# Second layer's gate and pooling weights: rounded by their transfer, low parts by an adding transfer

## The chip, the cores and the metric

One core of one Trainium2 chip runs the whole kernel. The metric is device microseconds of one execution; three runs of the kernel before gave a median of 670.25 us (670.14 to 670.65).

## What is computed

A trunk of two encoder layers on a sequence of 512 tokens with 1024 channels, in float32, and a last RMSNorm. Cut to what matters here:

```python
def hybrid_layer(x, ...):
    h = rmsnorm(x, norm_w)
    proj = jnp.einsum('bsd,de->bse', h, w_in)          # 1024 -> 4608 columns
    aq, ak, av, ag, bq, bk, bv, bg, cu, cg = jnp.split(proj, splits, axis=-1)
    o_a = diff_attention(aq, ak, av, ...) * silu(ag)   # 4 heads
    o_b = retention(bq, bk, bv, ...) * silu(bg)        # 4 heads
    o_c = multiscale_pool(cu, ...) * silu(cg)          # 4 channel groups
    return x + jnp.concatenate([o_a, o_b, o_c], -1) @ w_out
```

The columns of the gates bg and cg and of the pooling input cu are, of each layer's input weights, those from 3072 to 4608, twelve blocks of 128 columns.

## The kernel before, in words

**Split numbers.** TensorE multiplies in a rounded 32-bit format (fp32r). So that no precision is lost, each operand is kept as two tiles, a rounded high part and a low part, which is the value less its high part. `split` (L451) makes them: ScalarE rounds the source into the high tile, then VectorE subtracts that from the source into the low tile. `mm3` (L496) is then three matmuls, high by high, high by low and low by high.

**Weights.** `weight_granules` (L38) lists all weights in the order in which they are used, in granules of 128 partitions by 1024 floats (512 KB); one granule is 8 blocks of 128 by 128 for a column block of the input projection. `emit_granule` (L427) takes the next one: SyncE loads it into a raw tile (`wraw`, two buffers), and `split` makes `wh` and `wl` (five buffers each, `WBUFS`, L25). `take` (L443) hands granules out and keeps five emitted ahead, so a granule reuses the buffer of one about five before it, once TensorE is done with that. A raw load needs only a raw tile, so it can run before the weight buffer is free; a raw tile is free again when VectorE has subtracted.

**Use.** `proj_T` (L512) takes one granule and runs 24 matmuls (8 blocks by three) into one of three PSUM banks called `pj`. `gate` (L769) makes a gate from such a bank with ScalarE and VectorE. `c_pool` (L899) copies a bank to a tile `u`, whose margins GpSimd fills with zeros, and makes window sums of it on VectorE. `b_qk` and `b_head` are the retention heads; `headnorm` (L535) raises a row of means to the power -1/2 on GpSimd, sends it through DRAM and scales by it.

**Order.** `ORDERS` (L32) gives the units of each layer by hand; of the second it begins "bv bg0 cu0 bqk0 cg0 bqk1 B0 bg1 cg3 Cy0 cg2 cu1 cu2 cu3 cg1 Cy2 Cy1 bg2 B1 bg3 oT0". Instructions are first recorded in that order. Then `schedule` (L220) simulates five engines with the durations of `cost` (L323) and the delays of `LATENCY` (L162): each engine takes, of what can start at its next free moment, the instruction of the best priority, which is its place in the record less a boost (`HIGH`, L59: +300 for bqk, -20 for cu and cg, -300 for bg). Tiles and banks of a tag are given out in the order of the record, so a unit can hold a bank before it runs. The result is one fixed order for each engine, down to single matmuls, and on the chip each engine keeps it and waits by semaphores. Units therefore mix: eight matmuls of cu0 run first in the second layer, then bqk0's 24 break in, and bg0 runs late.

All instructions are issued from one line, L1055, so the views tell them apart by the tiles they write and read (`wl<-wraw,wh` is a weight's subtraction, `wh<-wraw` its rounding, `pj<-hh,wh` a projection's matmul).

Of the kernel before, what the change touches and what calls it, by code (L numbers as in the profile page):

```python
# [9 lines left out]
F32 = mybir.dt.float32  # L10
F32R = mybir.dt.float32r
AF = mybir.ActivationFunctionType
ALU = mybir.AluOpType
# [10 lines left out]
AQ, AK, AV, AG, BQ, BK, BV, BG, CU, CG = 0, 512, 1024, 1536, 2048, 2304, 2560, 3072, 3584, 4096  # L24
WBUFS = 5  # L25
# [12 lines left out]
def weight_granules():  # L38

    out = []  # L40
    for l in range(DEPTH):
        for u in ORDERS[l]:
            if u in ("bv", "av"):
                out += [("w_in", l, (256 * g, BV if u == "bv" else AV), (2, 512)) for g in range(4)]
                continue
            kind, i = u[:-1], int(u[-1])
            if kind in ("bg", "ag", "cu", "cg"):
                out.append(("w_in", l, (0, {"bg": BG, "ag": AG, "cu": CU, "cg": CG}[kind] + i * P), (8, P)))
            elif kind in ("bqk", "qk"):
                out += [("w_in", l, (0, c + i * P), (8, P)) for c in ((BQ, BK) if kind == "bqk" else (AQ, AK))]  # L50
            elif kind[0] == "o":
                out += [("w_out", l, ("PQRSTU".index(c) * 256, 512 * i), (2, 512)) for c in kind[1:]]
    return out
# [5 lines left out]
HIGH = {"A": 3000, "Am": 300, "B": 3000, "t": 150, "av": -20, "qk": 60, "o": 150, "bqk": 300, "Cy": 2000, "cu": -20, "bg": -300, "cg": -20, "ag": -20}  # L59
# [110 lines left out]
class Recorder:  # L170
# [9 lines left out]
    def add(self, name, engine, method, args, kw):  # L180
        op = Op()
        op.engine, op.method, op.args, op.kw = engine, (name, method), args, kw
        op.prio, op.unit = len(self.ops) - self.boost, self.unit
        outs = [args[0]] + ([kw["accum_out"]] if "accum_out" in kw else [])
        ins = [v for v in list(args[1:]) + [x for k, x in kw.items() if k != "accum_out"] if isinstance(v, View)]
        deps, bases = {}, []
        for views, write in ((ins, False), (outs, True)):
            for v in views:
                if not isinstance(v, View):
                    continue  # L190
                b, m = v.base, v.mask()
                if b not in bases:
                    bases.append(b)

                def hits(entries):
                    return [e for e in entries if e[1] < v.p1 and v.p0 < e[2] and e[3] & m]

                for e in hits(b.writes) + (hits(b.reads) if write else []):
                    if e[0] is not op:
                        deps[id(e[0])] = e[0]  # L200
                entry = (op, v.p0, v.p1, m)
                if write:
                    def covered(e):
                        return v.p0 <= e[1] and e[2] <= v.p1 and not e[3] & ~m and e[0] is not op
                    b.writes = [e for e in b.writes if not covered(e)] + [entry]
                    b.reads = [e for e in b.reads if not covered(e)]
                else:
                    b.reads.append(entry)
        if engine == "PE":
            b = outs[0].base  # L210
            if b.chain is not None:
                deps[id(b.chain)] = b.chain
            b.chain = op
        for b in bases:
            b.left += 1
        op.bases, op.deps, op.users = bases, list(deps.values()), []
        op.time, op.hold = cost(engine, method, args, kw)
        self.ops.append(op)

# [103 lines left out]
def cost(engine, method, args, kw):  # L323

    out = args[0]
    n = out.idx.size if isinstance(out, View) else 0
    psum = any(isinstance(a, View) and a.base.space == "psum" for a in args)
    if engine == "PE":
        if method == "transpose":
            return 109, 109  # L330
        f32 = args[1].base.dt == F32 and not any(s[0] == "bitcast" for s in args[1].steps)
        if f32:
            return 2 * 110 + 4 * n * 0.417, 2 * 110 + 4 * n * 0.417
        t = max(107, n * 0.417) + 2.5
        return t, t
    if engine == "SP":
        nbytes = (out.p1 - out.p0) * n * 4 if isinstance(out, View) and out.base.space != "dram" else P * D * 4
        if isinstance(out, View) and out.base.space == "dram":
            nbytes = 16384
        return nbytes / 360.0, 475  # L340
    if engine == "DVE":
        if method == "tensor_tensor":
            t = 1.041 * n + 69
        elif method == "scalar_tensor_tensor":
            t = 1.041 * n + (130 if isinstance(args[2], View) else 69)
        elif method == "tensor_scalar":
            t = (1.17 if psum else 0.64) * n + 69
        elif method == "tensor_copy":
            t = (1.04 if psum else 0.521) * n + 68
        elif method == "reciprocal":  # L350
            t = 6.2 * n + 69
        elif method == "memset":
            t = 9
        else:
            t = 1.041 * max(n, 2) + 75
        return t, t
    if engine == "ACT":
        t = 0.833 * n + (52 if psum else 94)
        for k in ("bias", "scale"):
            t += 93 * isinstance(kw.get(k), View)  # L360
        t += 93 * ("accum_out" in kw)
        return t, t
    if method == "tensor_tensor" and kw["op"] == ALU.pow:
        return 300 + 164 * n, 300 + 164 * n
    if method == "tensor_tensor":
        return 60 + 2.2 * n, 60 + 2.2 * n
    return 60 + 1.3 * n, 60 + 1.3 * n


def record(ins: dict, out: bass.AP):  # L370
    nc = Recorder()
    x_d = ins["x"][0]

    def sb(tag, shape, bufs=1, dt=F32, name=None):
        return nc.tile("sb", tag, shape, bufs, dt)
# [45 lines left out]


    granules = [(i, shape) for i, (_, _, _, shape) in enumerate(weight_granules())]
    wt = []
    wstate = [0]

    def emit_granule(parts=1):  # L427
        at, (nk, nc_) = granules[len(wt)]
        shp = [P, nk, nc_]
        src = ins["wg"][at].rearrange("p (k c) -> p k c", k=nk)  # L430
        raw = sb("wraw", shp, 2)
        hi = sb("wh", shp, WBUFS, F32R)
        lo = sb("wl", shp, WBUFS, F32R)
        n = shp[1] // parts
        for i in range(parts):
            k = slice(i * n, (i + 1) * n)
            was, nc.boost = nc.boost, HIGH.get("w", 0)
            nc.sync.dma_start(raw[:, k, :], src[:, k, :])
            split(hi[:, k, :], lo[:, k, :], raw[:, k, :])
            nc.boost = was  # L440
        wt.append((hi, lo))

    def take(n):  # L443
        i = wstate[0]
        wstate[0] += n
        while len(wt) < min(i + WBUFS, len(granules)):
            emit_granule()
        return wt[i:i + n]


    def split(dh, dl, src):  # L451
        nc.scalar.copy(dh, src)
        nc.vector.tensor_tensor(dl, src, dh.bitcast(F32), op=ALU.subtract)
# [227 lines left out]
    class Layer:  # L681
# [18 lines left out]
        def first_values(self):  # L700
# [10 lines left out]
            for u in START.split():  # L711
                i = int(u[1:] or 0)
                if u[0] == "k":
# [5 lines left out]
                    if i % 2 == 0:  # L719
                        emit_granule(2 if i < FINE else 1)  # L720
# [316 lines left out]
@with_exitstack  # L1037
def trunk(ctx: ExitStack, tc: tile.TileContext, ins: dict, out: bass.AP):
    pools = {
        "sb": ctx.enter_context(tc.tile_pool(name="sb", bufs=1)),  # L1040
        "psum": ctx.enter_context(tc.tile_pool(name="ps", bufs=1, space=bass.MemoryType.PSUM)),
        "dram": ctx.enter_context(tc.tile_pool(name="dr", bufs=1, space=bass.MemoryType.DRAM)),
    }
    with tc.manual_schedule():
        for op in record(ins, out).schedule():
            for b in op.bases:
                if b.real is None:
                    name = f"{b.tag}_{b.slot}"
                    b.real = pools[b.space].tile(b.shape, b.dt, tag=name, bufs=1, name=name)

            def real(v):
                return v.resolve() if isinstance(v, View) else v

            name, method = op.method
            op.inst = getattr(getattr(tc.nc, name), method)(*[real(a) for a in op.args], **{k: real(v) for k, v in op.kw.items()})  # L1055
# [67 lines left out]
```

## Time and profile before

| | us |
|---|---|
| median of three runs | 670.25 |
| the profiled execution | 670.98 |
| its span, from first to last instruction | 669.2 |
| TensorE busy in the span | 657.1 |
| VectorE busy | 478.3 |
| ScalarE busy | 385.2 |
| GpSimd busy | 30.2 |

Times in the views count from the span's start. PE is TensorE's matmuls, DVE is VectorE, ACT ScalarE, POOL GpSimd, SPq the queue that SyncE issues transfers from. Matmuls are pipelined: one begins 0.23 us after the other though each lasts 0.39, so a stall is read from the distance of two starts. The granted clock of TensorE is 0.999 of its 2.4 GHz over the whole span.

### The profile page before, as it was taken

The numbers are of one execution on the slowest core, as the hardware profiler recorded it, in microseconds if no ns is written. First come the engines' busy times: TensorE is split into PE (matmuls) and PEld (weight loads), VectorE is DVE, ScalarE is ACT, GpSimd is POOL, SyncE is SP. The second block draws the span as 40 slices with busy tenths as digits, with TensorE's granted clock in tenths as the row PEclk, the third lists the DMA queues.
The fourth block names the chain that finished last, engine by engine and source line by source line (L and its number), as shares of the span: only waits on it lengthen the run. The fifth ranks groups of instructions, "written<-read, shape, count | busy, mean of one in ns | idle before, by whom it ended". The sixth has DMA issues, their size and how long they took to land. (4 is left out here: it accounts for less than half of the span.)

```text
span 669.2 us, 8859 instructions
## 1 busy us (share of the span) xinstructions
PE 657.1 (98%) x3173; PEld 538.0 (80%) x3173; DVE 478.3 (71%) x865; ACT 385.2 (58%) x735; POOL 30.2 (5%) x51
## 2 busy tenths in 40 slices
PE   8999999999999999999999999999999999999996
PEld 6887878887788888887888788778888878888885
DVE  5798886776788879875754878587558846887733
ACT  6646885534776776552524877244567756874321
POOL 0100000000000000001010000000100000000011
PEclk9999999999999999999999999999999999999999
DMA  8545454223234322244113414433331243212302
GB/s 309 202 153 165 116 153 111 95 97 103 66 102 122 116 80 63 91 114 123 64 64 111 141 64 96 121 121 84 80 111 59 69 134 109 92 63 81 110 31 95
DMA packets 29300, 71.59 MB, mean 107 GB/s; under 512 B 5460, under 2 KB 9716, under 8 KB 29256
## 3 DMA queue, kind: packets, MB, share of 16 engines
q1 hardware_dynamic: 29256, 71.02, 34.4%
q8 instruction: 25, 0.41, 0.3%
q14 instruction: 19, 0.16, 0.1%
HBM read 68.83 MB, written 2.18 MB: 106 GB/s over the span
## 5 line engine op out<-in xcount | busy, mean ns | idle before, releaser
L1055 PE MATMUL pj<-hh,wh 128*128 128x512 f32 x448 | 176.9, 398 | 2.1 <-DVE gate L1055 1.3
L1055 PE MATMUL pj<-hl,wh 128*128 128x512 f32 x448 | 176.4, 395 | 0.0
L1055 PE MATMUL pj<-hh,wl 128*128 128x512 f32 x448 | 176.0, 396 | 0.0
L1055 ACT CAST wh<-wraw 128x1024 fp32r<-128x1024 f32 (+1 forms) x97 | 100.8, 1039 | 84.3 <-PE pj L1055 65.5
L1055 DVE TENSOR_TENSOR wl<-wraw,wh 128x1024 fp32r<-128x1024 f32 (+1 forms) x97 | 117.3, 1209 | 35.0 <-ACT wh L1055 34.5
L1055 PEld LDWEIGHTS pj<-hh,wh 128*128 128x128 f32 x448 | 84.1, 188 | 21.8 <-DVE gate L1055 1.9
L1055 PEld LDWEIGHTS pj<-hh,wl 128*128 128x128 f32 x448 | 84.0, 188 | 18.3
L1055 PEld LDWEIGHTS pj<-hl,wh 128*128 128x128 f32 x448 | 84.2, 188 | 17.8
L1055 PE MATMUL pj<-wh,mAC 128*128 128x512 f32 (+1 forms) x264 | 86.8, 390 | 0.0
L1055 ACT ACTIVATE soft<-soft,sm 128x512 f32<-128x512 f32 x96 | 68.6, 721 | 21.8 <-DVE sm L1055 20.8
L1055 DVE TENSOR_TENSOR x<-x,pj 128x512 f32<-128x512 f32 (+1 forms) x65 | 43.8, 676 | 19.7 <-PE pj L1055 19.2
L1055 PEld LDWEIGHTS pj<-wh,mAC 128*128 128x128 f32 x264 | 48.8, 188 | 10.3 <-DVE mAC L1055 0.2
L1055 PE MATMUL pj<-wl,mAC 128*128 128x512 f32 (+1 forms) x132 | 51.5, 390 | 0.0
L1055 PE MATMUL lg<-qk 128*128 128x512 f32 (+1 forms) x192 | 50.3, 360 | 0.7 <-DVE soft L1055 0.4
L1055 DVE CUSTOM_DVE_ANT_0 soft<-lg,wide 128x512 f32<-128x512 f32 x64 | 43.1, 686 | 9.7 <-PE lg L1055 7.0
L1055 POOL TENSOR_TENSOR st<-st,neghalf 128x4 f32<-128x4 f32 (+1 forms) x28 | 25.0, 892 | 476.2 <-DVE st L1055 447.5
L1055 PE MATMUL pj<-wh,mB 128*128 128x512 f32 (+1 forms) x136 | 44.3, 382 | 0.0
L1055 PE MATMUL pj<-wh,hh 128*128 128x512 f32 x104 | 41.3, 397 | 0.4 <-DVE vl L1055 0.4
L1055 PE MATMUL pj<-wl,hh 128*128 128x512 f32 x104 | 41.4, 398 | 0.0
L1055 PE MATMUL pj<-wh,hl 128*128 128x512 f32 x104 | 41.1, 396 | 0.0
L1055 PEld LDWEIGHTS lg<-qk 128*128 128x128 f32 x192 | 32.5, 188 | 8.0 <-issue 1.5
L1055 PE MATMUL ov<-T,vh 128*128 128x256 f32 x192 | 38.8, 283 | 0.0
(156 smaller groups left out, 951.6 us busy)
## 6 DMA issues: line engine op xcount, KB each, us to landing
wraw<-in_wg SPq DMA_DIRECT2D x95, 512.0 KB, 3.3
hn<-row SPq DMA_DIRECT2D x16, 256.0 KB, 3.4
wide<-gd SPq DMA_DIRECT2D x8, 448.0 KB, 3.1
T<-in_xT_w SPq DMA_DIRECT2D x8, 258.0 KB, 4.9
x<-in_x SPq DMA_DIRECT2D x8, 256.0 KB, 5.2
wide<-dd SPq DMA_DIRECT2D x8, 256.0 KB, 5.1
out<-T SPq DMA_DIRECT2D x8, 256.0 KB, 2.1
qd<-dd SPq DMA_DIRECT2D x8, 128.0 KB, 4.5
```

Source lines behind the costliest of these rows:

```text
L1055: op.inst = getattr(getattr(tc.nc, name), method)(*[real(a) for a in op.args], **{k: real(v) for k, v in op.kw.items()})
```

## The change

For the twelve granules of the second layer with the gate columns bg and cg and the pooling columns cu, the raw tile falls away. GpSimd issues a transfer from DRAM straight into the high tile, which rounds. ScalarE copies the high tile, times -1, into the low tile. GpSimd then issues a second transfer of the same weights into the low tile, which adds to what lies there. VectorE's subtraction falls away. All other weights go as before, the attention gates ag among them.

The recorder learns that a transfer with `accum_op` also reads its target. The cost table gets an entry for GpSimd's transfers: 5300 ns until done and 600 ns of GpSimd, 7200 and 900 where it adds. The whole order is planned again with that.

```diff
+        kw_ins = [args[0]] if "accum_op" in kw else []
...
+    if engine == "POOL" and method == "dma_start":
+        return (7200, 900) if "accum_op" in kw else (5300, 600)
...
+    BYTRANSFER = [i for i, (name, l, (r, c), _) in enumerate(weight_granules()) if l == 1 and name == "w_in" and BG <= c < CG + 512]
...
+        if at in BYTRANSFER:
+
+            hi = sb("wh", shp, WBUFS, F32R)
+            lo = sb("wl", shp, WBUFS, F32R)
+            was, nc.boost = nc.boost, HIGH.get("w", 0)
+            nc.gpsimd.dma_start(hi, src)
+            nc.scalar.activation(lo, hi.bitcast(F32), AF.Copy, scale=-1.0)
+            nc.gpsimd.dma_start(lo, src, accum_op=ALU.add)
+            nc.boost = was
+            wt.append((hi, lo))
+            return
```

## Rows read from the trace of the kernel before

**Rows 1.** The page, part 1: busy us, share of the span and instructions of each engine.

```profile
PE 657.1 (98%) x3173; PEld 538.0 (80%) x3173; DVE 478.3 (71%) x865; ACT 385.2 (58%) x735; POOL 30.2 (5%) x51
```

**Rows 2.** Busy time by stretch: length, busy time of each engine (instructions), clock, DMA.

```profile
350.00:480.00 130.00, 127.37 (x612) 103.72 (x611) 87.19 (x127) 71.30 (x124) 3.47 (x9) 1.00 0.35 101
480.00:657.50 177.50, 176.63 (x854) 145.46 (x853) 121.83 (x235) 102.74 (x213) 8.77 (x9) 1.00 0.28 87
```

**Rows 3.** TensorE's order of time: start, us, operation, tiles, [idle before <- releaser].

```profile
368.20 0.40 PE L1055 MATMUL pj<-hl,wh 128*128 128x512 f32 x1
369.14 0.50 PE L1055 MATMUL pj<-hh,wh 128*128 128x512 f32 x1 [0.55 <-ACT soft L1055]
...
410.40 0.59 PE L1055 MATMUL lg<-qk 128*128 128x256 f32 x3 [0.40 <-DVE soft L1055]
...
426.59 0.39 PE L1055 MATMUL pj<-hh,wl 128*128 128x512 f32 x1
426.82 0.40 PE L1055 MATMUL pj<-hh,wh 128*128 128x512 f32 x1
428.54 0.50 PE L1055 MATMUL pj<-hh,wh 128*128 128x512 f32 x1 [1.32 <-DVE gate L1055]
...
435.11 0.40 PE L1055 MATMUL pj<-hh,wl 128*128 128x512 f32 x1
435.74 0.50 PE L1055 MATMUL pj<-hh,wh 128*128 128x512 f32 x1 [0.23 <-ACT u L1055]
```

**Rows 4.** Tile wl on VectorE, 350 to 480: ns least/median/most, first and last start.

```profile
L1055 DVE TENSOR_TENSOR wl<-wraw,wh x21: 1215/1225/1227, 354.7 to 479.2; 128x1024 fp32r<-128x1024 f32 x21
```

**Rows 5.** VectorE's order of time ahead of the gate that TensorE waits for.

```profile
426.06 1.22 DVE L1055 TENSOR_TENSOR wl<-wraw,wh 128x1024 fp32r<-128x1024 f32 x1
427.20 0.69 DVE L1055 TENSOR_TENSOR T<-soft,T 128x512 fp32r<-128x512 f32 x1
427.80 0.68 DVE L1055 SCALAR_TENSOR_TENSOR gate<-gate,pj 128x512 f32<-128x512 f32 x1
```

**Rows 6.** ScalarE's order of time.

```profile
353.62 1.05 ACT L1055 CAST wh<-wraw 128x1024 fp32r<-128x1024 f32 x1 [0.85 <-PE pj L1055]
...
366.10 0.62 ACT L1055 CAST pwh<-wraw 128x512 fp32r<-128x512 f32 x1 [3.19 <-DMA wraw<-in_pool_w]
...
434.15 1.05 ACT L1055 CAST wh<-wraw 128x1024 fp32r<-128x1024 f32 x1 [7.95 <-PE pj L1055]
435.11 0.58 ACT L1055 COPY u<-pj 128x512 f32<-128x512 f32 x1
```

**Rows 7.** Waits of SyncE's queue, 350 to 480: us in total, times, longest us.

```profile
SPq L1055 <- DVE wl L1055: 86.4, 19, 17.0
```

**Rows 8.** GpSimd's order of time, two of its powers.

```profile
412.80 1.02 POOL L1055 TENSOR_TENSOR st<-st,neghalf 128x4 f32<-128x4 f32 x1 [28.67 <-issue]
...
460.44 1.01 POOL L1055 TENSOR_TENSOR st<-st,neghalf 128x4 f32<-128x4 f32 x1 [13.26 <-DVE st L1055]
```

**Rows 9.** Transfers of the whole kernel: KB each, median us from issue to landing.

```profile
wraw<-in_wg SPq DMA_DIRECT2D x95, 512.0 KB, 3.3
...
sin<-in_c_sin SPq DMA_DIRECT2D x2, 256.0 KB, 6.6
```

**Rows 10.** SyncE's queue in order of time, one issue.

```profile
411.46 0.33 SPq L1055 DMA_DIRECT2D wraw<-in_wg  x1
```

**Rows 11.** TensorE's order of time at the granules cu0, bg0 and cg3.

```profile
353.14 0.40 PE L1055 MATMUL pj<-wh,hl 128*128 128x512 f32 x1
...
357.55 0.39 PE L1055 MATMUL pj<-hh,wh 128*128 128x512 f32 x1
...
375.04 0.39 PE L1055 MATMUL pj<-hh,wh 128*128 128x512 f32 x1
...
384.26 0.39 PE L1055 MATMUL pj<-hh,wl 128*128 128x512 f32 x1
...
400.13 0.65 PE L1055 MATMUL pj<-hh,wh 128*128 128x512 f32 x2
```

More of the change, by code (lines that the diff above doesn't have):

```diff
@@ L184, in add @@
         outs = [args[0]] + ([kw["accum_out"]] if "accum_out" in kw else [])
-        ins = [v for v in list(args[1:]) + [x for k, x in kw.items() if k != "accum_out"] if isinstance(v, View)]
+        kw_ins = [args[0]] if "accum_op" in kw else []
+        ins = [v for v in list(args[1:]) + [x for k, x in kw.items() if k != "accum_out"] + kw_ins if isinstance(v, View)]
         deps, bases = {}, []
```

## The prediction

> **What bounds the kernel now.** I read first the page's busy times: TensorE is busy for 98% of the span, VectorE for 71%, ScalarE for 58%, GpSimd for 5% [rows 1]. A busy TensorE need not be a full one, so the second view is the busy time by stretch. The weights that the change touches are used between 357 and some 475 us. Of the 130 us from 350 to 480, TensorE is busy 127.37; after that, to 657.5, it is busy 176.63 of 177.50 [rows 2]. There is almost nothing to win outside the first stretch. VectorE, which the change relieves, is busy 87.19 of the 130 us; it has 43 us to spare and bounds only where TensorE waits for it.
>
> The third view is TensorE's order of time, searched for late starts. Matmuls of 512 columns start every 0.23 us (426.59 to 426.82). Three starts of the stretch come later than that [rows 3]:
> - at 369.14, 0.94 after the one before, so 0.71 lost (released by ScalarE);
> - at 428.54, 1.72 after the one before, so 1.49 lost (released by VectorE);
> - at 435.74, 0.63 after the one before, so 0.40 lost (released by ScalarE).
>
> Together 2.60 us. A fourth, at 410.40, idles 0.40 for a VectorE operation of a retention head that no weight stands ahead of. So about 3.0 us can be had at most, under half a per cent of the kernel.
>
> **The change, part by part.** *VectorE loses* twelve subtractions of 1.225 us [rows 4], 14.7 us of busy time. They count only where TensorE ends up waiting behind one. For the 1.49 us, VectorE's order of time shows it: the subtraction at 426.06 is that of cg1, and a split and then the gate operation that TensorE waits for start behind it at 427.20 and 427.80 [rows 5]. Without it both start 1.14 earlier, and the wait shrinks by 1.14. Bounds: 0 to 1.49.
>
> *ScalarE keeps* twelve passes: instead of rounding 1024 columns into the high part it copies them, negated, into the low part; I cost both at the 1.05 us of the rows [rows 6]. What moves is their place: the pass now waits for the first transfer into the weight tile, which itself waits until the buffer is free. At 434.15 ScalarE rounds bg2 the moment its buffer comes free, and the copy of cu1's result that TensorE's bank waits for stands behind it at 435.11. That pass moves at least 3 us later, and the 0.40 goes (bounds 0 to 0.40). At 366.10 ScalarE has just waited 3.19 us for the raw load of the pooling matrices; the copies that TensorE waits for at 369.14 stand behind that. The load waits for one of two raw tiles: SyncE's queue waits 86.4 us in this stretch for VectorE to be done with them [rows 7]. The twelve granules no longer use raw tiles, so this load comes early, and the 0.71 goes (bounds 0 to 0.71).
>
> *SyncE loses* twelve loads; its queue only gets shorter. *GpSimd gains* 24 transfers on an instruction queue that is served in order: behind an adding transfer that waits for ScalarE stand the margin fills of the next pooling input and the powers of the head norms, which VectorE waits for. It has little else to do here; a power takes 1.01 or 1.02 us [rows 8]. A fill that is held up by some 2 us delays a pooling chain, not TensorE: there are three banks, and the one that the pooling input came from is wanted again two granules, 11 us, later. I cost it at 0; with that cover gone it costs the delay itself.
>
> *The new chain.* Before, a raw load ran ahead of the buffer's release, and one pass on ScalarE and one on VectorE (2.3 us) came after it. Now all of it comes after: issue, transfer, ScalarE, issue, adding transfer. No row shows a GpSimd transfer. For an issue, the nearest rows are 0.33 us (a load on SyncE's queue [rows 10]) and 1.01 (GpSimd's power); I take 1.0, as that is GpSimd's own. For the first transfer, 3.3 (the 512 KB weight loads) to 6.6 (the slowest kind of load) [rows 9]; I take 3.3, the same bytes into the same kind of tile. For the adding one, which also reads 512 KB back from the tile, 3.3 to 9.9 (6.6 + 3.3); I take twice 3.3. Sum: 1.0 + 3.3 + 1.05 + 1.0 + 6.6 = 12.95, and four handovers of 0.1 (TensorE's matmul of 353.14 ends at 353.54, ScalarE begins at 353.62 [rows 6, 11]): 13.4 us. Ends: 0.33 + 3.3 + 1.05 + 0.33 + 3.3 = 8.3, and 1.0 + 6.6 + 1.05 + 1.0 + 9.9 = 19.6.
>
> The Trainium skill ("DMA: Bandwidth & Descriptors", section "Anatomy of one DMA — SWDGE (gpsimd) path") fits a transfer issued by GpSimd as 2.0 us plus its bytes over 436 GB/s, which makes an estimate of 3.2 us for 512 KB, without a price for adding. By it the first term would be 3.2 in place of 3.3, and the sum the same; no run so far shows such a transfer.
>
> *Its cover.* Counting 24 matmuls to a granule along TensorE's order, the twelve granules have 19 us or more from the release of their buffer to their first use, but for two. For cg3 it is 15.7 (its buffer's last matmul, at 384.26, ends at 384.65; its own first is the second of the two from 400.13, at about 400.35). For cu0 it is 4.0: its buffer is free at 353.54, its first matmul at 357.55 [rows 11]. A chain of 13.4 is far too late for that. But the planner counts transfers as long and takes up what is ready: bg0, whose buffer was free well before 350 and which holds a bank, though it runs only from 375.04 now; and bqk0, which now breaks into cu0 after eight matmuls. That is 48 matmuls, 11.0 us, so cu0's low part is not missed before 368.6: a cover of 15.1 us. The 13.4 fit under 15.1 and 15.7.
>
> *Sum.* Gains 0.71 + 1.14 + 0.40 = 2.25. ScalarE gets twelve new waits for first transfers, where the plan puts their landing: the one wait of 3.19 seen here cost 0.71, and I take a third of that once, 0.25 (0 to 0.71). Net 2.0 us. The profiled execution took 670.98 with a span of 669.2, so 1.78 lie outside it: 669.2 - 2.0 + 1.78 = 668.98. The median of the runs is 0.73 under the profiled execution: 668.25, so **668.3 us**.
>
> **The rivals.** About 0.2%, 1.34 us, is what a measurement of this kernel can tell from no change, so faster means under 668.9 and slower over 671.6.
>
> 1. *The stalls move.* The whole order is planned anew, and TensorE's small stalls depend on which operation stands ahead of which; new neighbours take back what the old ones gave. For it: VectorE has 43 us idle, and TensorE waits all the same. Against: all three stalls have a cause by name that the change takes away. Time: 2.25 gone, about as much come back, 670.2, within 669.0 and 671.5.
> 2. *The chain outgrows its cover*, at cu0 and cg3. The stalls are (chain - 15.1) + (chain - 15.7). They use up the 2.25 at a chain of 16.5 us, and from 17.2 the kernel is slower by over 0.2%. At 18.4, the middle between that and the upper end: 3.3 + 2.7 - 2.25 = 3.75, so 674.0; at the upper end 4.5 + 3.9 - 2.25, so 676.4. For it: no row has an adding transfer, which could be slower than two loads. Against: 13.4 from the nearest rows.
> 3. *GpSimd's issues wait for VectorE.* If the VectorE operation in progress held up each issue, two waits of up to 1.23 make the chain 15.9: cu0 is 0.8 late and cg3 0.2, so -2.0 + 1.0, 669.2. Against: the power takes the same 1.01 and 1.02 us wherever it lies [rows 8]. The Trainium skill ("SBUF — State Buffer", section "SBUF: two separate sides") warns that GpSimd cannot write descriptors while VectorE runs in a mode that takes both of its ports; for operations with two inputs in SBUF, as nearly all are here, it names only GpSimd's reads as held up.
>
> **How the numbers follow.** Forecast 47%, rival 1 29%, rival 2 20%, rival 3 4%. The forecast's own range is 667.2 (all 3.0 gone) to 668.9. The range starts at 666.9, as another 0.3 may come from the 0.87 us after 480; about 5% lie below. It ends at 673.0, which takes in rivals 1 and 3 and the lower part of rival 2; some 14% lie above. Faster 0.47; same 0.33 (rivals 1 and 3); slower 0.20 (rival 2).
>
> **What would show it.** VectorE has 85 weight subtractions instead of 97 and 14.7 us less. TensorE runs bg0 ahead of cu0 at 357.6, and no start near 369, 428 and 436 is over 0.3 late. From a buffer's release to the end of the adding transfer it is under 15 us, and TensorE waits for no weight tile. I am wrong if TensorE waits for a GpSimd transfer at cu0 or cg3, if ScalarE waits long for first transfers with banks held behind it, or if new late starts of the same size stand elsewhere.

## The result, and the profile after

The changed kernel is slower: 676.34 us (median of 6 executions, 674.04 to 677.78) against 670.58 (6 executions on the same chip, 670.14 to 672.85), a ratio of 1.0076 with a 95% interval of 1.0052 to 1.0099. Its profiled execution took 676.97 us with a span of 675.2, 6.0 more than before.

The page of the changed kernel, parts 1, 3 and 6 (columns as in [rows 1] and [rows 9]; of part 3: packets, MB, share of 16 engines' span). All its instructions are issued from L1071.

```profile
PE 658.7 (98%) x3173; PEld 539.1 (80%) x3173; DVE 465.5 (69%) x853; ACT 384.6 (57%) x735; POOL 46.8 (7%) x75
...
q0 software_dynamic: 3456, 12.58, 8.2%
...
wh<-in_wg POOLq DMA_DIRECT2D x12, 512.0 KB, 4.6
wl<-in_wg POOLq DMA_DIRECT2D x12, 512.0 KB, 6.1
...
wide<-dd SPq DMA_DIRECT2D x8, 256.0 KB, 4.6
```

VectorE has twelve instructions less (865 to 853), and the page's group of weight subtractions falls from 117.3 to 102.6 us. So the relief came in full, and it bought nothing. The windows of the changed kernel say where to look, in the form of [rows 2]:

```profile
350.00:480.00 130.00, 123.50 (x587) 100.19 (x586) 74.01 (x114) 68.65 (x120) 19.34 (x31) 0.99 0.58 140
480.00:657.50 177.50, 176.53 (x852) 145.16 (x851) 121.20 (x233) 104.55 (x214) 8.20 (x8) 1.00 0.27 88
```

TensorE loses 3.87 us of busy time in the first stretch and 0.10 in the second; the DMA engines' busy share there goes from 0.35 to 0.58, though the bytes per second only go from 101 to 140. TensorE's order of time in the changed kernel, its late starts and one ordinary matmul ahead of the first (columns as in [rows 3]):

```profile
367.39 0.40 PE L1071 MATMUL pj<-hh,wl 128*128 128x512 f32 x1
368.61 0.50 PE L1071 MATMUL pj<-hh,wl 128*128 128x512 f32 x1 [0.81 <-DMA wl<-in_wg]
...
400.45 0.50 PE L1071 MATMUL pj<-hh,wh 128*128 128x512 f32 x1 [0.71 <-DVE gate L1071]
...
414.67 0.59 PE L1071 MATMUL lg<-qk 128*128 128x256 f32 x3 [1.38 <-DVE soft L1071]
...
423.62 0.74 PE L1071 MATMUL lg<-qk 128*128 128x256 f32 x4 [2.19 <-DVE soft L1071]
...
451.66 0.50 PE L1071 MATMUL pj<-hh,wh 128*128 128x512 f32 x1 [1.41 <-ACT u L1071]
```

Reckoned as in the prediction, by the distance of two starts less the usual one, these lose 0.98, 0.88, 1.54, 2.35 and 1.57 us, together 7.3. In the kernel before the stretch lost 3.5: the 2.6 of the forecast's three stalls, 0.65 at 410.40 and 0.29 at a start at 418.61. In this execution none of the three old ones is left at its place. Five others came:

- 0.98 at 368.61: cu0's low part. This is rival 2, in small. In a second profiled execution (a_full, the last experiment) it doesn't show, and 0.49 is lost at 369.52 instead.
- 0.88 and 1.57 at 400.45 and 451.66: an operation of the new order that stands too far ahead of its supplier. The planner's own simulation has both holes, with 1.02 and 1.80 us. This is rival 1.
- 1.54 and 2.35 at 414.67 and 423.62: two logits (`lg`) of the retention heads. Nothing in the prediction led there.

The last matmul starts 5.20 us later than before (668.16 against 662.96): 3.8 from the late starts of this stretch, 0.3 less elsewhere, and 1.7 because TensorE ran at the lower of its two clocks, 1.2 GHz, for one piece of 3.42 us:

```profile
424.97:428.39 3.42, 3.42 (x10) 2.65 (x10) 2.61 (x4) 1.48 (x2) 0.87 (x1) 0.50 0.90 122
```

The other 0.8 us lie behind the last matmul, in the end of the kernel (7.05 us there in place of 6.24, and the same 7.05 or 7.06 in every kernel that keeps the new order). The clock piece turned out to be no cost of the change (below, at the last experiment).

**What the heads wait for.** Each retention head masks its logits with a table of decays (`wide<-dd`, 256 KB) that SyncE loads for it. There is one buffer, so the next load is issued when VectorE has used the last one, and a load that lands late makes the next head late. In the kernel before, SyncE's issues and VectorE's first operation behind each load, in order of time:

```profile
405.23 0.38 SPq L1055 DMA_DIRECT2D wide<-dd  x1
409.56 0.69 DVE L1055 SCALAR_TENSOR_TENSOR soft<-lg,wide 128x512 f32<-128x512 f32 x1 [1.07 <-DMA wide<-dd]
...
413.29 0.38 SPq L1055 DMA_DIRECT2D wide<-dd  x1
417.77 1.29 DVE L1055 SCALAR_TENSOR_TENSOR soft<-lg,wide 128x512 f32<-128x512 f32 x2 [0.60 <-DMA wide<-dd]
```

From issue to use 4.3 and 4.5 us. In the changed kernel, the chain that ended last (start, us, what) and then the order of time:

```profile
358.75 9.81 DMA wl<-in_wg
...
407.88 5.93 DMA wide<-dd
...
416.59 6.19 DMA wide<-dd
```

```profile
409.02 0.89 POOL L1071 DMA_DIRECT2D wl<-in_wg  x1 [8.30 <-ACT wl L1071]
412.20 1.84 POOL L1071 DMA_DIRECT2D wl<-in_wg  x2 [2.30 <-ACT wl L1071]
...
413.83 0.69 DVE L1071 SCALAR_TENSOR_TENSOR soft<-lg,wide 128x512 f32<-128x512 f32 x1 [1.68 <-DMA wide<-dd]
...
422.87 1.29 DVE L1071 SCALAR_TENSOR_TENSOR soft<-lg,wide 128x512 f32<-128x512 f32 x2 [2.52 <-DMA wide<-dd]
...
429.74 1.29 DVE L1071 SCALAR_TENSOR_TENSOR soft<-lg,wide 128x512 f32<-128x512 f32 x2 [2.11 <-DMA wide<-dd]
```

The same loads take 5.9 and 6.2 us, and a third, issued at 424.19, 5.5 (5.1 before, where nothing waited for it). Three adding transfers go out beside the first two loads. While the second load is out, from 416.59 to 422.87, GpSimd's queue alone takes most of the 16 engines (part 3 of the page for that window: packets, MB, share):

```profile
q0 software_dynamic: 336, 1.21, 84.4%
q1 hardware_dynamic: 416, 0.26, 19.0%
```

The packet records of the trace show what that does: the load's first packet starts 3.5 us after its issue, while that of the load of 405.23 in the kernel before starts 1.0 us after. In part 4 of the page, the chain that ended last, the loads `wide<-dd` hold 2% of the span by themselves.

### The profile page after: what moved, and what is told of

Same layout as the page of the kernel before. It is cut to its first block, busy times and chain, and to the rows that moved or that the text cites. A ratio compares the mean times of both kernels' runs of the same rounds, so it can differ in the third digit from the quotient of the medians.

```text
span 675.2 us, 8863 instructions
## 1 busy us (share of the span) xinstructions
PE 658.7 (98%) x3173; PEld 539.1 (80%) x3173; DVE 465.5 (69%) x853; ACT 384.6 (57%) x735; POOL 46.8 (7%) x75
## 4 chain that ended last, share of the span: by engine, by line
PE 71%; issue 16%; DMA 5%; DVE 3%; ACT 3%; POOL 1%; POOLq 0%; ACTq 0%; DVEq 0%; SPq 0%
PE pj L1071 58%; PE lg L1071 6%; PE ov L1071 4%; PE tp L1071 4%; DMA wide<-dd 2%; DMA wl<-in_wg 1%; DVE soft L1071 1%; ACT soft L1071 1%; ACT qk L1071 1%; POOL st L1071 1%; DMA hn<-row 1%; ACT T L1071 1%; DMA wide<-gd 0%; DVE T L1071 0%; DVE qk L1071 0%
## 5 line engine op out<-in xcount | busy, mean ns | idle before, releaser
L1071 PE MATMUL pj<-hh,wh 128*128 128x512 f32 x448 | 177.4, 398 | 2.1 <-ACT u L1071 1.4
L1071 PE MATMUL pj<-hh,wl 128*128 128x512 f32 x448 | 176.9, 398 | 0.8 <-DMA wl<-in_wg 0.8
L1071 PE MATMUL pj<-hl,wh 128*128 128x512 f32 x448 | 177.0, 397 | 0.0
L1071 ACT CAST wh<-wraw 128x1024 fp32r<-128x1024 f32 (+1 forms) x85 | 88.1, 1037 | 70.5 <-PE pj L1071 53.4
L1071 DVE TENSOR_TENSOR wl<-wraw,wh 128x1024 fp32r<-128x1024 f32 (+1 forms) x85 | 102.6, 1208 | 28.1 <-ACT wh L1071 27.5
L1071 PEld LDWEIGHTS pj<-hh,wh 128*128 128x128 f32 x448 | 84.5, 189 | 21.7 <-ACT u L1071 2.3
L1071 PEld LDWEIGHTS pj<-hh,wl 128*128 128x128 f32 x448 | 84.4, 189 | 19.4 <-DMA wl<-in_wg 1.3
L1071 PEld LDWEIGHTS pj<-hl,wh 128*128 128x128 f32 x448 | 84.6, 189 | 17.7
L1071 PE MATMUL pj<-wh,mAC 128*128 128x512 f32 (+1 forms) x264 | 86.9, 391 | 0.0
L1071 ACT ACTIVATE soft<-soft,sm 128x512 f32<-128x512 f32 x96 | 68.6, 721 | 21.6 <-DVE sm L1071 20.6
L1071 DVE TENSOR_TENSOR x<-x,pj 128x512 f32<-128x512 f32 (+1 forms) x65 | 43.8, 676 | 20.8 <-PE pj L1071 20.3
L1071 PEld LDWEIGHTS pj<-wh,mAC 128*128 128x128 f32 x264 | 48.8, 188 | 10.6 <-DVE mAC L1071 0.3
L1071 POOL TENSOR_TENSOR st<-st,neghalf 128x4 f32<-128x4 f32 (+1 forms) x28 | 24.1, 861 | 449.5 <-DVE st L1071 446.1
L1071 PE MATMUL lg<-qk 128*128 128x512 f32 (+1 forms) x192 | 50.6, 360 | 3.7 <-DVE soft L1071 3.6
L1071 PE MATMUL pj<-wl,mAC 128*128 128x512 f32 (+1 forms) x132 | 51.7, 392 | 0.0
L1071 DVE CUSTOM_DVE_ANT_0 soft<-lg,wide 128x512 f32<-128x512 f32 x64 | 43.1, 686 | 9.7 <-PE lg L1071 7.0
L1071 PE MATMUL pj<-wh,mB 128*128 128x512 f32 (+1 forms) x136 | 44.3, 382 | 0.0
L1071 PE MATMUL pj<-wh,hh 128*128 128x512 f32 x104 | 41.4, 398 | 0.4 <-DVE vl L1071 0.4
L1071 PEld LDWEIGHTS lg<-qk 128*128 128x128 f32 x192 | 32.5, 188 | 11.4 <-issue 2.9
L1071 PE MATMUL pj<-wl,hh 128*128 128x512 f32 x104 | 41.3, 397 | 0.0
L1071 PE MATMUL pj<-wh,hl 128*128 128x512 f32 x104 | 41.1, 396 | 0.0
L1071 PE MATMUL ov<-T,vh 128*128 128x256 f32 x192 | 38.8, 283 | 0.0
```

## Experiments

Two theories stood against each other. The order theory (A): the new plan places TensorE's work badly, and the transfers themselves are harmless. The transfer theory (B): the new transfers take the 16 DMA engines from loads that TensorE waits for; in its sharper form (B1) it is the adding ones, because adding is dear. The kernels ran in three groups, each on one chip, beside executions of the kernel before on the same chip (medians of those: 672.65, 673.33 and 673.24 us). Ratios are against these, with 95% intervals.

**The order of before, with the new transfers (order_b).** The instructions of the kernel before keep its order on every engine; eleven granules (cu0 is left as it was) get the three new instructions in place of their load, rounding and subtraction.

```diff
-    order = record(ins, out).schedule()
+    order = merged(ins, out)   # order of before; a granule's transfers go in where its buffer comes free
```

> Eleven of the twelve granules (all but cu0) go by GpSimd's two transfers, but every engine keeps the order of the kernel before: TensorE's, VectorE's less eleven subtractions, ScalarE's with the copy put 5.6 us of planned time after the buffer's release. Theory A (the new order is what costs): no new holes, two of the old late starts go, 668 to 670.5 us beside 670.5 of before. Theory B (the transfers are what cost, since they slow the decay-table loads that the retention heads wait for, from 4.3 and 4.5 us to 5.9 and 6.2): the heads' two waits of 1.54 and 2.35 stay although the order is the old one, 673 to 676. Theory C (the chain outgrows its cover): cu0 left out, so 0.98 less than the changed kernel, 675.

Measured: 678.94 us, 1.0098 (1.0075 to 1.0120), above what any of the theories expected. The order of before doesn't bring the time back: a loss of this size needs no new order, and a decay load is late here too. Its order of time on VectorE, TensorE and ScalarE:

```profile
412.16 0.69 DVE L1108 SCALAR_TENSOR_TENSOR soft<-lg,wide 128x512 f32<-128x512 f32 x1 [2.33 <-DMA wide<-dd]
...
412.99 0.71 PE L1108 MATMUL lg<-qk 128*128 128x256 f32 x4 [2.24 <-DVE soft L1108]
...
441.62 1.06 ACT L1108 ACTIVATE wl<-wh 128x1024 fp32r<-128x1024 f32 x1 [3.49 <-DMA wh<-in_wg]
...
446.38 1.06 ACT L1108 ACTIVATE wl<-wh 128x1024 fp32r<-128x1024 f32 x1 [3.22 <-DMA wh<-in_wg]
...
453.95 0.50 PE L1108 MATMUL pj<-mAC,pwh 128*128 128x512 f32 x1 [3.44 <-ACT mAC L1108]
```

The decay load that ends at 412.16 was issued at 404.45 and took 7.7 us, with adding transfers issued at 403.00, 405.66 and 408.36. The second loss is another: ScalarE keeps its order and stands twice for over 3 us before a first transfer; a pooling chain starts late behind that, and TensorE waits 3.44 for its last copy. Two pieces of 3.41 us at the lower clock, from 414.10 and 455.05, are in the time as well. So the total is no measure of the decay loads alone.

**The adding transfer cut to an eighth (a_add8).** The order of the changed kernel is kept exactly; the transfer adds only the first of the 8 blocks, so seven eighths of these low parts are left as the negated high part.

```diff
+            if "accum_op" in op.kw:
+                op.args = [v[:, 0:1, :] for v in op.args]
```

> The changed kernel in its own order, but each adding transfer moves and adds the first of eight blocks alone (seven eighths of the low parts keep the negated high part, so this computes something else). Theory A (order): only cu0's wait of 0.98 goes, 674.5 to 676. Theory B (traffic of the adding transfers slows the decay-table loads): these land in under 5 us again, the heads' waits shrink from 3.9 to about 1 and the stretch at half clock goes, 671 to 672.5. Theory C (the adding transfer is too long): cu0's wait goes, 675 to 675.5.

Measured: 673.87 us, 1.0016 (1.0001 to 1.0031). The order, the first transfers and the number of instructions are the same. cu0's wait is gone, the heads' waits are 0.29 and 0.89 (1.54 and 2.35 in the change), and the decay loads take 4.7, 4.8 and 4.6 us. The two holes of the plan stay, 0.88 and 1.57. It changes nothing but the bytes that are added. The ratio makes the gain look larger than it is: ten of the 25 executions of the kernel before on this chip have a mean granted clock of 0.996 or less, and none of these ten. Among executions at 0.997 or more (those of the kernel before take 672.32 at 0.997 and 672.06 at 0.998, but 674.57 at 0.996) it takes 673.87 against 672.06, 1.8 us longer; the change, on the third chip, takes 3.7 longer (675.96 against 672.29). So about half of the loss is gone.

**The adding transfer without adding (a_addplain).** Order and bytes of the changed kernel; the second transfer overwrites instead of adding, so the low parts hold the rounded weights themselves.

```diff
+            op.kw.pop("accum_op", None)
```

> The changed kernel in its own order, with the second transfer of each granule a plain one of the same bytes: nothing is added, so the low tile ends up as the weights themselves (this computes something else). Theory B1 (adding is what is dear: its 4 KB packets took 328 ns on their DMA engine, a plain transfer's some 160 to 174): between the cut-down kernel and the full change, 0.2 to 0.45% over before, decay loads after 5 us or less. Theory B2 (twelve more transfers of 512 KB are dear, adding or not): as the full change, 0.65 to 0.9%. Theory A (the new order's two holes): 0.65% or more, as the order is the same.

Measured: 674.49 us, 1.0029 (1.0008 to 1.0050). Its page, parts 3 and 6:

```profile
q0 software_dynamic: 3456, 12.58, 6.1%
...
wl<-in_wg POOLq DMA_DIRECT2D x12, 512.0 KB, 3.9
```

The same packets and bytes as in the change take 6.1% of 16 engines' span instead of 8.2%. Over the two spans that is 656 and 886 us of engine time, 230 us more for the 1536 packets that add (twelve transfers of 128 packets of 4 KB): 0.15 us each. The packets' own records agree: a median of 0.33 us for one that adds and 0.17 for one that doesn't; 0.16 for a packet of SyncE's weight loads in the kernel before. The windows from 404 to 432 us show it as occupation, of the kernel before, the change, this kernel and a_add8 in turn (the last two columns are the DMA share and GB/s):

```profile
404.00:432.00 28.00, 26.15 (x145) 21.74 (x145) 20.09 (x31) 14.56 (x29) 1.02 (x1) 1.00 0.47 119
```

```profile
404.00:432.00 28.00, 24.43 (x136) 20.69 (x136) 18.30 (x30) 18.48 (x34) 5.73 (x7) 0.94 0.79 157
```

```profile
404.00:432.00 28.00, 26.10 (x151) 22.23 (x150) 18.21 (x30) 18.26 (x34) 4.28 (x7) 1.00 0.67 175
```

```profile
404.00:432.00 28.00, 27.14 (x156) 22.86 (x155) 19.50 (x32) 18.60 (x34) 5.74 (x7) 1.00 0.54 116
```

The change moves fewer bytes per second than this kernel and keeps the engines busier. The heads' waits follow the kind of transfer: 3.9 us with adding (1.54 + 2.35), 2.2 without (0.69 + 1.53), 1.2 with an eighth (0.29 + 0.89), at one and the same order. They are the load's time and nothing else: in the change, a_full, this kernel and a_add8 the first wait is the time from issue to use of its load (5.9, 6.0, 5.1 and 4.7 us) less 4.4, the second (6.3, 6.4, 5.5 and 4.8) less 3.9.

The same chip ran the change once more (a_full, below): 677.13, 2.6 us above this kernel, and 1.7 above it among executions with a mean clock of 0.997 or more (675.96 against 674.22). So B1, that adding is what is dear, holds for about half of the loss. The rest is not divided by an experiment: at 0.997 or more this kernel is 1.9 us above the kernel before and a_add8 1.8, so the seven eighths of plain bytes between them make no difference that can be told, and both keep the plan's holes and its longer end. Single traces give an account of it: the late starts of the stretch come to 7.0 us in a_full, 4.7 here and 3.6 in a_add8, against 3.5 before, and the end is 0.8 longer in all three. That makes 4.3, 2.0 and 0.9 us beside the measured 3.7, 1.9 and 1.8.

**Part of the granules (a_first3, a_late9).** Only bg0, cu0 and cg0 by transfer, and only the other nine. Both are planned anew.

```diff
-... if l == 1 and name == "w_in" and BG <= c < CG + 512]
+... if l == 1 and name == "w_in" and BG <= c < CG + 512 and c in (BG, CU, CG)]      # a_first3
+... if l == 1 and name == "w_in" and BG <= c < CG + 512 and c not in (BG, CU, CG)]  # a_late9
```

> The changed kernel with only bg0, cu0 and cg0 by transfer; their adding transfers are over by some 375 us, before the heads' decay loads after 400. Theory B: no late decay load, so the time of the kernel before, within 0.2% (the plan has one hole of 0.7 us, cu0 may wait 1 us as in the changed kernel, and 1 or 2 us of the old waits may go): 0.998 to 1.002. Theory C (chain at cu0): cu0's wait of about 1 us is all that is lost. Theory A: holes from bg0 being used up early, up to 0.4% slower.

> The changed kernel without these three: the nine later granules by transfer. Theory B: the adding transfers of cg3, cg2, cu1, cu2 and cu3 still meet the heads, 0.5 to 1.0% slower than before. Theory A with bg0 and cu0 as the cause: as fast as before, within 0.2% (but this plan has two holes of 1.5 us, so up to 0.45% slower). Theory C: no wait at cu0, 0.1% less than the changed kernel.

Measured: 673.18 us, 0.9999 (0.9981 to 1.0017), and 677.61 us, 1.0070 (1.0044 to 1.0095). The three whose transfers end before the heads cost nothing that can be told, the nine around the heads about as much as all twelve. TensorE and VectorE in order of time in a_late9:

```profile
419.43 1.29 DVE L1071 SCALAR_TENSOR_TENSOR soft<-lg,wide 128x512 f32<-128x512 f32 x2 [5.15 <-DMA wide<-dd]
...
420.17 0.73 PE L1071 MATMUL lg<-qk 128*128 128x256 f32 x4 [3.35 <-DVE soft L1071]
```

That load was issued at 412.53 and took 6.9 us. The pair is less clean than it looks, on both sides. In a_late9 the heads' two waits are 0.93 and 3.51, but the plan of this kernel has two holes of its own (1.45 and 1.58 in the planner's simulation), and TensorE loses about 1.3 at each of them, at 455.79 and 457.46. So the heads are only about half of its 8.7 us of late starts.

And the one profiled execution of a_first3 (674.76 us, the longest of its ten) has heads' waits of 1.69 and 2.25 too, with decay loads of 5.1 and 5.7 us and no transfer of GpSimd's in flight. Beside the first of them one of SyncE's own weight loads is on the engines; in the last microsecond before the second is used, hardly a packet moves, and that stays unexplained. So waits of that size come without GpSimd's transfers as well. They cost little here because this plan closes the old stalls at 428 and 436: its late starts are 4.8 us (these two and 0.89 at 395.22) against 3.5 before, and this execution also has a piece of 3.41 us at the lower clock.

**A second buffer for the decay table (a_decay2, and b_decay2 as its control).** Every other head of the second layer loads its table into a tile of its own, in the changed kernel and in the kernel before.

```diff
+        if row >= 4 and row % 2:
+            t = sb("rb", [P, S]).rearrange("p (j c) -> p j c", j=2)
+        else:
             t = sb("wide", [P, 896], 1)[:, 0:512].rearrange("p (j c) -> p j c", j=2)
```

> The changed kernel, in which the second layer's odd retention heads load their decay table into a second buffer, so a load no longer waits for the head before. Both theory A and B put 1.54 + 2.35 of TensorE's waits and the 3.4 us at half clock (1.7) on these loads: if they are the cause, 5 us go and 670.5 to 671.5 is left, with the hole of 0.88 still there; the plan closes the other (1.57) by itself here, which would make it 669 to 670. Theory C (chain of the weights): 675 to 676.

> The kernel before with the same second buffer, as the control: its late starts at the heads are 0.62 and 0.29 (410.4 and 418.6), so at most 0.9 us go, and the plan moves others a little: 669.3 to 670.6. If it gains as much as the changed kernel does, the second buffer is not about the change.

Measured: 676.36 us, 1.0051 (1.0028 to 1.0073), and 672.80 us, 0.9997 (0.9978 to 1.0017). The control costs and gains nothing. In the changed kernel I had expected nearly all of the loss back; the interval overlaps that of the change. What is gone in the trace is the hole of 1.57, which this plan closes by itself. The heads' waits of 3.9 are gone too, but one of 4.1 at 430.25 came in their place, for a gate that stands on VectorE behind a head's masking. Its order of time and its list of issues between 350 and 480 say why:

```profile
413.82 0.87 POOL L1074 DMA_DIRECT2D wl<-in_wg  x1 [2.29 <-ACT wl L1074]
415.31 0.88 POOL L1074 DMA_DIRECT2D wl<-in_wg  x1 [0.61 <-DVE T L1074]
...
425.46 0.69 DVE L1074 SCALAR_TENSOR_TENSOR soft<-lg,rb 128x512 f32<-128x512 f32 x1 [5.73 <-DMA rb<-dd]
```

```profile
rb<-dd SPq DMA_DIRECT2D x1, 256.0 KB, 10.9
```

The load could go out earlier, at 414.40, and for that it went out right between two adding transfers and took 10.9 us. So the single buffer is not the cause of the late load. One of the ten executions, the only one with a mean clock above 0.996, took 672.40; no profile of it shows whether its load was late.

**Transfers added to the kernel before (b_junkadd, b_junkcopy).** For the same twelve granules GpSimd also loads their weights in two halves into a tile that nobody reads, adding or plain.

```diff
+                nc.gpsimd.tensor_copy(junk[:, 0:1], hi[:, 0, 0:1].bitcast(F32))
+                for h in range(2):
+                    nc.gpsimd.dma_start(junk.rearrange("p (k c) -> p k c", k=4), src[:, 4 * h:4 * h + 4, :], accum_op=ALU.add)
```

> The kernel before in its own order, with its own weight chain, and besides, for each of the twelve granules, two adding GpSimd transfers of half a granule into a tile that nobody reads, issued when ScalarE has rounded the granule. Theory B (adding transfers hold the DMA engines, and the retention heads' decay tables arrive late): the decay loads after 400 us take 5.5 us or more in place of 4.3 and 4.5, TensorE's waits at the heads grow by 1.5 to 4 us, 0.3 to 1.0% slower than before. Theory A (order) and C (chain): no change within 0.2%.

> The same kernel with plain GpSimd transfers of the same bytes in place of the adding ones. If it is the adding (packets of 4 KB took 328 ns each in the changed kernel against some 160 to 174 for plain ones), about half or less of the loss is left, up to 0.3%. If any GpSimd traffic does it, as slow as with adding. Theory A and C: no change.

Measured: 696.08 us, 1.0342 (1.0308 to 1.0377), and 678.08 us, 1.0088 (1.0063 to 1.0114), both far above what was expected. Adding is much worse than plain, but this pair is not clean. The waits of b_junkadd (us in total, times, longest):

```profile
POOL rb L1065 <- DMA rb<-in_wg: 81.7, 19, 7.1
...
DVE hn L1065 <- POOL u L1065: 12.9, 2, 7.8
```

GpSimd waits for its own transfers, because all go into one tile, and the margin fills and powers of the pooling units stand queued behind. Plain, the first wait is 59.6 us and the second 3.6. In the profile of b_junkadd TensorE also runs 17.1 us at its lower clock, which is up to 8.5 us lost. How the 23 us divide between a queue held up, that clock and full DMA engines isn't shown, and the pair is left out of the argument.

**Only cg1 and bg2 by transfer (a_cg1bg2).** These are the two granules whose subtraction and rounding the prediction found ahead of the late starts at 428.54 and 435.74.

```diff
+... if l == 1 and name == "w_in" and c in (CG + P, BG + 2 * P)]
```

> Only cg1 and bg2 go by transfer, the two granules whose passes stood ahead of the gate and the copy that TensorE waited for at 428.5 and 435.7 (1.48 and 0.39 us); their transfers start after the heads' last decay load, and the plan has no hole. Theory B: those waits go and nothing new comes, 1.2 to 2 us less than before, 0.997 to 0.9985. Theory A (any new plan moves the stalls): within 0.2% of before on either side.

Measured: 673.09 us, 1.0007 (0.9987 to 1.0028): no gain, against an expected one. The 0.40 at 435.74 is gone. Of the 1.49, this is left, in order of time on VectorE and TensorE:

```profile
424.49 1.29 DVE L1071 SCALAR_TENSOR_TENSOR soft<-lg,wide 128x512 f32<-128x512 f32 x2 [0.65 <-DMA wide<-dd]
425.69 0.68 DVE L1071 SCALAR_TENSOR_TENSOR gate<-gate,pj 128x512 f32<-128x512 f32 x1
...
426.43 0.50 PE L1071 MATMUL pj<-hh,wh 128*128 128x512 f32 x1 [1.87 <-DVE gate L1071]
```

The subtraction of [rows 5] is out of the way, the gate operation starts 2.1 earlier than before (425.69 against 427.80), and TensorE waits 1.87 for it instead of 1.32. It also came to that place earlier, since its matmul before starts at 424.16 instead of 426.82. The gate now stands right behind a head's masking of 1.29 us, which itself idles 0.65 for a decay load. So with the subtraction gone, the next work of the heads in VectorE's order sets the wait.

**The change once more (a_full).** The unchanged changed kernel, as an anchor on the third chip.

> The changed kernel once more, as the anchor on the same chip as the other two: 0.5 to 1.0% over before by all theories; TensorE's two waits at the heads 3 us or more together, with decay loads of 5.5 us and more.

Measured: 677.13 us, 1.0064 (1.0043 to 1.0086). Heads' waits of 1.61 and 2.45, decay loads of 6.0, 6.4 and 5.1 us, and in its windows no piece at the lower clock:

```profile
350.00:480.00 130.00, 123.81 (x595) 100.47 (x594) 74.09 (x114) 68.80 (x120) 19.35 (x31) 1.00 0.58 142
```

cu0's wait is not there, but a late start near 369 is, 0.49 lost. On ScalarE and TensorE:

```profile
365.10 1.06 ACT L1071 ACTIVATE wl<-wh 128x1024 fp32r<-128x1024 f32 x1 [4.20 <-DMA wh<-in_wg]
...
367.12 2.35 ACT L1071 COPY soft<-pj 32x512 f32<-32x512 f32 x4
...
369.52 0.50 PE L1071 MATMUL pj<-hh,wh 128*128 128x512 f32 x1 [0.33 <-ACT soft L1071]
```

The copies that TensorE waited for at 369.14 before stood behind the load of the pooling matrices. Now they stand behind a negated copy that waits 4.20 us for a first transfer. In the first profile of the change the same copy waits 3.97, hidden by cu0's wait.

This bears on the clock. Executions of both kernels have mean granted clocks from 0.993 to 0.999; the profiled executions with one piece of 3.4 us at the lower clock stand at 0.994 to 0.996, those with none at 0.998 or 0.999. On this chip, at 0.998 or more, the medians are 672.5 us before (7 executions) and 676.0 after (4); at 0.996 or less 673.7 (16) and 678.0 (5). The change costs 3.5 and 4.3 us: much the same at either clock. And the lower values are as frequent in both, 16 of 28 executions before and 5 of 9 after. So the clock piece is no cost of the change.

## Why the prediction was wrong

**What held.** VectorE's twelve subtractions went, with the 14.7 us forecast. bg0 ran ahead of cu0 (at 356.70, with two of cu0's matmuls and then bqk0's mixed in). The late starts at 428 and 436 are gone from their places. GpSimd's queue cost the other engines nothing that the list of waits shows: between 350 and 480 none waits for a fill or a power. The chain for a weight tile was forecast at 13.4 us. From issue to landing the first transfer takes 4.1 (median of those between 350 and 480; 3.5 to 6.8), the negated copy 1.06, the adding transfer 6.3 (5.2 to 9.8): 11.5 and the handovers. The estimates of 1.0 + 3.3 and 1.0 + 6.6 were close, both a little high. But the two transfers don't follow each other at once: from the issue of the first to the landing of the second the eleven granules took 11.1 to 21.2 us, 14.6 in the median, and at least five of them more than the 15 that the prediction gave as its sign, because GpSimd waits for ScalarE's copy where the plan has put it. At cu0, with a 9.81 us adding transfer, the chain was 15.9 from the buffer's release, 0.8 over the cover of 15.1, and TensorE waited 0.81 for it; cg3 did not wait. So rival 2 had its place right and was small. That the measured 676.34 lies beside its upper end of 676.4 is chance: that end needs 4.5 us lost at cu0 and 3.9 at cg3, and 0.98 and nothing were.

The Trainium skill ("DMA: Bandwidth & Descriptors", section "Anatomy of one DMA — SWDGE (gpsimd) path") gives a fit by which a 512 KB transfer is estimated at 3.2 us; none of the first transfers of the changed kernel was that fast (3.5 at least).

**The 1.14 of cg1's subtraction** was wrong in its own right. VectorE's queue was read correctly, but I took the time between the subtraction and the gate as what would be won. TensorE came to the wait earlier too, and the next thing in line, a head's masking, kept it there (a_cg1bg2). A wait on a chain with several links shrinks only to the next link.

**The 0.71 at 369** was credited to one wait of ScalarE's, and that wait did go: the load of the pooling matrices comes early. A wait for a first transfer took its place, 3.97 and 4.20 us, and left 0.49 in one of two executions (a_full).

**Rival 1** held in size: 2.6 us of old stalls went in the first profile, and two holes of the new plan, 0.88 and 1.57, took back 2.45. All three kernels with this order (the change, a_addplain and a_add8) have them. That much would have given no change, but for the 0.8 us that the new order adds behind the last matmul.

**The step that failed** is the sentence on the queues: "SyncE loses twelve loads; its queue only gets shorter". I priced what the 24 new transfers do to the instructions queued behind them on GpSimd, and at what time they land, but not what they do to other transfers in flight. SyncE's queue did get shorter; the engines behind it got fuller. The planner makes the same omission: `schedule` lets SyncE's transfers take turns on one `bus`, and gives GpSimd's a fixed time beside it. Before, a granule's weights crossed the DMA engines once, at 0.16 us a packet; now twice, at 0.17 and 0.33, three times the occupation. The loads that suffered are those with no slack: the decay tables, one after the other, each wanted as soon as it lands. Their waits on TensorE went from 0.9 to 3.9 us, 3.0 of the 3.8 us by which the stretch's late starts grew. Without adding they were 2.2, with an eighth of it 1.2. The trace had it beforehand: the fourth late start, at 410.40 [rows 3], which the prediction set aside as one "that no weight stands ahead of", waits for VectorE, and VectorE for a decay load.

The Trainium skill states the rule ("DMA: Bandwidth & Descriptors", section "Issuing engines are not separate DMA queues"): transfers from different issuing engines end up on the same 16 DMA engines and interleave there. The traces agree: the loads that SyncE issues are slowed beside GpSimd's adding ones, from 4.3 and 4.5 us to between 5.9 and 7.7, and once to 10.9.

**ScalarE's new waits**, which I costed at 0.25, cost 0.49 in one profile of the changed kernel and are hidden in the other. With the order of before, TensorE waits 3.4 us at one place for a chain that starts behind them (order_b).

**What stays open.** How the loss divides between the first, rounding transfers and the second ones at zero added bytes wasn't tried; a_add8 bounds the first kind, with the holes of the plan and its longer end, at 1.8 us among executions at like clocks. About half of the change's loss is shown to come from adding (a_addplain against a_full); the other half is accounted for in traces, by the longer end of the new order and what is left of the heads' waits, but no run divides it. Why the second decay load of a_first3 is used late without any such transfer near is not explained. No kernel tried was faster than the kernel before; the nearest, b_decay2, a_first3 and a_cg1bg2, can't be told from it.

## What to carry to other kernels

A transfer that takes over an engine's work is priced three times: what it waits for, who waits for it, and which loads share the DMA engines while it runs; look above all for small loads in a chain with one buffer, where a consumer already waits. An adding transfer held the DMA engines for as long as two plain ones here. And before a stall is credited to the instruction ahead of it, look at what stands behind that one: the gain is only the distance to the next link.

## What the runs showed of the hardware

- In the changed kernel a 4 KB packet that adds into SBUF holds its DMA engine for 0.33 us, one that only rounds 0.17, a plain one of SyncE's 0.16 (medians of the packet records; the shares of a_addplain and the change give 0.15 for the difference between adding and not).
- A 256 KB load of SyncE's that went out between two adding transfers of 512 KB took 10.9 us (a_decay2), where 4.3 and 4.5 were taken before.
- GpSimd's issue of a transfer takes 0.53 to 0.62 us in the changed kernel between 350 and 480, and 0.87 to 0.90 where it adds, beside a VectorE that is busy for 57% of that stretch: rival 3 did not show.
- TensorE's clock fell to 1.2 GHz for a piece of 3.4 us in the profiles of the change, a_first3 and a_decay2, for two such pieces in order_b, and for none in those of the kernel before, a_full, a_add8 and a_addplain. A piece began 1.4 us after a late start that had lost 2.35 us in the change, and 1.1 us after one of 2.49 in order_b; after 2.45 in a_full, 2.79 in b_decay2 and 3.51 in a_late9 the clock did not fall, so the length of the wait alone doesn't tell.
